# The merge of dilated attention: a power and all additions on GpSimd, and another place for the rows' tiles

## The chip, the core and the metric

The kernel runs on one core of a Trainium2 chip. A core has five engines that work at the same time, each through its own queue of instructions: TensorE (PE: matrix products; PEld is its loading of weights, which overlaps them), VectorE (DVE), ScalarE (ACT), GpSimd (POOL) and SyncE (SP, which here only issues DMA transfers). They share an on-chip memory of 128 partitions, in which every tile has its bytes in each partition; matrix products land in a separate small memory (PSUM), and DMA engines move data between the chip's memory and the main one. An instruction that needs another engine's result, or a buffer that another still uses, waits on a semaphore, and all that stands behind it in its engine's queue waits with it.

The metric is the time of one execution of the program on the device, in microseconds; lower is better.

## What is computed

One inference step of a hybrid decoder layer, for one prompt of 2048 tokens and for 32 sample tokens (8 requests of 4) that share its weights:

```python
a = rmsnorm(h); [qa|fa|ia|ga|qb|kb|vb] = a @ w_in
h = h + concat(HGRN2(qa,fa,ia,ga), DilatedAttn(qb,kb,vb)) @ w_o
h = h + ConvFFN(rmsnorm(h))
h = h + sigmoid(rmsnorm(h) @ w_ple_gate) * (p @ w_ple_proj)
```

The part at hand is the prompt's attention: 8 heads of 64 features, and three dilations (window, step): (128, 1), (512, 4) and (2048, 16). Each dilation gives, for every query, a maximum m of its scores, a sum l of their exponentials and a weighted sum acc of the values. They are combined so:

```python
w = exp(ms - ms.max(axis=0))
return (w[..., None] * accs).sum(0) / (w * ls).sum(0)[..., None]
```

## The kernel before

**Stages.** First the input projection, in two blocks of tokens, with the recurrent units (HGRN) between them; then the prompt's attention with the samples' work beside it; then the trunk (output projection, ConvFFN and embedding gate), in three blocks of tokens. The trunk's products are made of three matrix products each (lines 143 to 145), of weights and activations split into a rounded half and a remainder.

**The prompt's attention** (`attn_phase`). The heads are taken in four pairs, p = 0 to 3. The kernel folds the three dilations into two parts, di = 0 and di = 1, with a mask of counted entries, so two results per query are to be merged. A part of a pair has four chunks c of 512 tokens, a chunk four blocks of 128 queries, and a block one or two units. A unit makes scores (L811 and L812 on TensorE), adds the mask and finds the smallest sum (L816, one VectorE instruction; the sign is turned, so a smallest one stands for the maximum), takes exponentials on ACT (L817), turns them by transposes (L824), copies these out of PSUM (L826, on VectorE or for every fourth unit on ACT), and multiplies with the values (L836). When a chunk of a part is complete, ACT copies the result out of PSUM into a buffer `o0` or `o1`, five of each (L886).

TensorE's order in this stage is written out by hand: a loop over x steps through the units, and what is late by so many units is called at x - 3, x - 7 and so on. Between the units stands, every second turn, a piece of the samples' work (`others`), which reads 32 pieces of the cached keys and values of 1 MB each (tiles `skt`, L940 and L976).

**The next pair's data.** SP loads chunks of queries and keys into one of four `stage` buffers (L690). POOL rounds and subtracts them into `qS` (L701 and L149) and, after ACT has made `kH` (L704), into `kL` (L705). For p > 0 this happens about ten units before the pair begins.

**The merge** (`merge`, L740 to L775), once for each pair and chunk, 16 times in all, in six pieces that are called 0, 2, 3, 7, 10 and 11 turns after the chunk's second part. (1) SP loads the statistics of the first part back (L742). (2) VectorE takes the smaller of the two extremes (L750), POOL subtracts (L751), ACT takes exponentials (L752). (3) POOL multiplies and adds (L754, L755), VectorE takes the reciprocal of 128 x 8 values (L756), POOL multiplies (L757). (4) TensorE turns the coefficients (L760), ACT copies them out (L762), SP writes them to memory (L763) and loads them again, spread over the partitions, as `cf` (L767, two loads). (5) POOL multiplies the two results, 128 x 512 each, by their coefficients (L772). (6) The two are added (L774), by VectorE for p < 3 and by POOL for p = 3, and SP writes the sum to `mix_d` (L775).

**The seam to the trunk.** The trunk's first block loads pieces of w_o in halves, 128 x 512 each, into seven buffers `raw` (L1004). ACT rounds each (L181), VectorE makes the remainder (L182). The activations h are read from `mix_d` (L1098) and split the same way, by ACT in L1080 and VectorE in L1081. The weights are asked for first in each group of the program.

**What sets the order elsewhere.** Except for TensorE in the attention, a planner orders each engine's queue when the program is built, by a timeline that it computes itself. SP's queue is among those.

**Where tiles lie.** Pools are stacked in the on-chip memory in the order in which they are opened, and a pool that is closed gives its bytes to the next one opened. With `reuse_waits="tile"` a new tile waits only for the last users of those older tiles on whose bytes it lies. In front of all lies `const`, up to byte 4352 of a partition. Then come `early` (8448 bytes, with the mask from byte 6656 to 9728) and `rows` (two tiles of 4224 bytes, `ssq` and `rb`, used by the input projection's norm alone). Both are closed when attention ends. On their bytes the trunk opens `ffn_c` (the convolution's constants, 1952 bytes) and then `tr`, the seven `raw` buffers of 2048 bytes.

Of the kernel before, what the change touches and what calls it, by code (L numbers as in the profile page):

```python
# [11 lines left out]
F32 = mybir.dt.float32  # L12
# [4 lines left out]
ALU = mybir.AluOpType  # L17
# [30 lines left out]
def hymba_step_kernel(ctx: ExitStack, tc: tile.TileContext, I: dict, O: dict):  # L48
    nc = tc.nc
    V, A, G, PE, SP = nc.vector, nc.scalar, nc.gpsimd, nc.tensor, nc.sync  # L50

    const = ctx.enter_context(tc.tile_pool(name="const", bufs=1))
    dram = ctx.enter_context(tc.tile_pool(name="scratch", bufs=1, space=DRAM))

    early_st = ExitStack()
    early = early_st.enter_context(tc.tile_pool(name="early", bufs=1, reuse_waits="tile"))

# [15 lines left out]
    ones = const.tile([128, 128], F32, name="ones")  # L73
    V.memset(ones, 1.0)

    mask = early.tile([128, 768], F32, name="mask")
    qT_s = early.tile([128, 4, NS], F32, name="qT_s")
    kT_s = early.tile([128, 4, NS], F32, name="kT_s")
# [603 lines left out]
    def attn_phase(spare, rest):  # L682
# [57 lines left out]
        def merge(p, c, parts, both):  # L740

            SP.dma_start(both[:, 0].rearrange("p n h c -> p n (h c)"),  # L742
                         stats_d[p][512 * c:512 * c + 512].rearrange("(n i) c -> i n c", i=128))
            stats = both.rearrange("p i n h c -> p c h i n")
            spread = lambda x: x.rearrange("p h (o n) -> p h o n", o=1).to_broadcast([128, 2, 2, 4])
            yield
            mn = sm.tile([128, 2, 4], F32, name="mn")
            w = sm.tile([128, 2, 2, 4], F32, name="w")
            wl = sm.tile([128, 2, 2, 4], F32, name="wl")
            V.tensor_reduce(mn, both.rearrange("p i n h c -> p c h n i")[:, 1], axis=mybir.AxisListType.X, op=ALU.min)  # L750
            G.tensor_sub(w, spread(mn), stats[:, 1])  # L751
            A.activation(w, w, AF.Exp)  # L752
            yield
            G.tensor_mul(wl, w, stats[:, 0])  # L754
            G.tensor_add(mn, wl[:, :, 0], wl[:, :, 1])  # L755
            V.reciprocal(mn, mn)  # L756
            G.tensor_mul(w, w, spread(mn))  # L757
            yield
            ptr = pT.tile([128, 4, 128], F32, name="PT")[:16, 0]
            PE.transpose(ptr, w.rearrange("p h d n -> p (h d n)"), ident)  # L760
            wt = sm.tile([16, 128], F32, name="wt")
            A.copy(wt, ptr)  # L762
            SP.dma_start(coef_d[p][c], wt)  # L763

            cf = wk.tile([128, 2, 512], F32, name="cf", bufs=2)
            for h in range(2):
                SP.dma_start(cf[64 * h:64 * h + 64].rearrange("p d i -> p (d i)"),  # L767
                             coef_d[p][c][8 * h:8 * h + 8].rearrange("(o r) i -> o (r i)", o=1)
                             .to_broadcast([64, 1024]))
            yield  # L770
            for i in range(2):
                G.tensor_mul(parts[i], parts[i], cf[:, i])  # L772
            yield
            (G if p == 3 else V).tensor_add(parts[1], parts[1], parts[0])  # L774
            SP.dma_start(mix_d[:, 4 + p, 512 * c:512 * c + 512], parts[1])  # L775

        class Block:
# [71 lines left out]
        n = len(units)  # L849
# [5 lines left out]
        def merge_at(xs, *args):  # L855
            gen = merge(*args)
            for x in xs:
                at(x, lambda: next(gen, None))
# [702 lines left out]
    def step(gen, n):  # L1561
        for _ in range(n):
            if next(gen, "end") == "end":
                return False
        return True

    def pools(st, **kw):
        def pool(name, bufs, **k):
            return st.enter_context(tc.tile_pool(name=name, bufs=bufs, reuse_waits="tile", **kw, **k))
        return pool  # L1570

    rows_st, in_st, hgrn_st, attn_st = [ExitStack() for _ in range(4)]
    rows = pools(rows_st)("rows", 1)
    pool = pools(in_st)
    args = (in_tiles(pool("xp", 1), rows), [], pool("wp", 9), pool("ev", 2), pool("sm", 1),
            pool("pmm", 2, space=PSUM), pool("pms", 2, space=PSUM))
# [80 lines left out]
        first(side, 1000)  # L1657
    step(main, 1000)
    attn_st.close()
    rows_st.close()  # L1660

    early_st.close()
    with ExitStack() as st:
        pool = pools(st)
        cp = pool("ffn_c", 1)
# [153 lines left out]
```

## Time and profile before

| | us |
|---|---|
| time, median of 3 runs | 3003.89 (3002.21 to 3005.41) |
| the profiled execution: its own time | 3008.49 |
| the profiled execution: its span | 3006.7 |
| TensorE's mean granted clock in it | 0.981 of full speed |
| TensorE busy, 0 to 830 us (input projection, HGRN) | 798.0 of 830 |
| TensorE busy, 830 to 1200 us (attention, samples) | 336.2 of 370 |
| TensorE busy, 1200 to 3006 us (trunk) | 1774.7 of 1806 |

The profile is of one execution, taken by the hardware's profiler. Its span runs from the first to the last instruction; the execution's own time lies around it. Times of single instructions come from this execution, and "idle time" of an engine is set down with what ended it: the instruction or the transfer that released the semaphore last. An idle time of an engine that is not the bottleneck costs nothing by itself. The granted clock is what the throttle left to TensorE, as a share of full speed. The loss of 33.8 us in the attention's stretch is made of many short gaps, not of one.

### The profile page before, as it was taken

To read this page: it belongs to the slowest core of one execution; us is meant where nothing else is said; L and a number is where in the kernel's file an instruction comes from. 1 tells how busy PE (TensorE), PEld (TensorE's weight loads), DVE (VectorE), ACT (ScalarE), POOL (GpSimd) and SP (SyncE) were. 2 spreads that over 40 slices of the span, in tenths; PEclk is the share of its full clock that TensorE was granted. 3 is DMA by queue.
4 is the path that set the end of the run, shared out by engine and by line. 5 is a ranking of instruction groups with operands and counts; after the bars stand their busy time and mean duration, and the time that the engine had idled before them with its cause. 6 is when DMAs were issued, how large, how long until landed. Compare 5 with 4: busy or idle time off the path is not lost.

```text
span 3006.7 us, 52441 instructions
## 1 busy us (share of the span) xinstructions
PE 2908.9 (97%) x18895; PEld 2711.0 (90%) x18895; DVE 2166.4 (72%) x4717; ACT 1319.2 (44%) x2856; POOL 676.9 (23%) x792
## 2 busy tenths in 40 slices
PE   8999999999989998999999999999999999999998
PEld 8987789887777677999999999999999999999997
DVE  6656768657386567569988889766769777777777
ACT  5333433222176666335444444544444544444453
POOL 1443222212143463102344431000001000000000
PEclk9999999999989999999999999999999999999998
DMA  5898634323349996766666568677779777778773
GB/s 183 297 359 299 202 103 120 99 86 121 122 107 286 276 249 177 260 224 220 224 206 196 191 198 302 227 252 250 246 230 321 240 242 246 257 249 295 269 274 131
DMA packets 343061, 664.14 MB, mean 221 GB/s; under 512 B 62929, under 2 KB 130641, under 8 KB 341009
## 3 DMA queue, kind: packets, MB, share of 16 engines
q1 hardware_dynamic: 305952, 472.68, 48.4%
q0 software_dynamic: 33264, 121.13, 12.6%
q10 hardware_dynamic: 3584, 66.98, 6.1%
q8 instruction: 149, 2.44, 0.3%
q14 instruction: 112, 0.91, 0.1%
HBM read 513.72 MB, written 213.92 MB: 242 GB/s over the span
## 4 chain that ended last, share of the span: by engine, by line
PE 78%; DVE 9%; DMA 7%; issue 2%; ACT 2%; POOL 1%; SPq 1%; DVEq 0%; POOLq 0%; ACTq 0%
PE mm L143 19%; PE mm L144 19%; PE mm L145 19%; PE mm L345 2%; PE mm L346 2%; PE mm L347 2%; PE acc L836 2%; PE PT L824 2%; PE S L811 1%; DVE h L1305 1%; PE S L812 1%; PE lv L482 1%; DMA wraw<-in_w_in_dram 1%; DMA cf<-coef_d 1%; DMA draw<-in_w_down_dram 1%
## 5 line engine op out<-in xcount | busy, mean ns | idle before, releaser
L144 PE MATMUL mm<-w 128*128 128x348 f32 (+3 forms) x3636 | 1167.6, 322 | 1.9 <-DVE w L1081 1.1
L143 PE MATMUL mm<-w 128*128 128x348 f32 (+3 forms) x3508 | 1111.4, 323 | 21.2 <-ACT s L1247 6.7
L145 PE MATMUL mm<-w 128*128 128x348 f32 (+3 forms) x3508 | 1118.9, 322 | 0.7 <-DVE w L182 0.7
L144 PEld LDWEIGHTS mm<-w 128*128 128x128 f32 x3636 | 685.4, 189 | 4.9 <-DVE w L1081 3.0
L143 PEld LDWEIGHTS mm<-w 128*128 128x128 f32 x3508 | 658.2, 189 | 29.7 <-ACT s L1247 9.3
L145 PEld LDWEIGHTS mm<-w 128*128 128x128 f32 x3508 | 660.2, 189 | 1.8 <-DVE w L182 1.0
L182 DVE TENSOR_TENSOR w<-raw,w 128x512 fp32r<-128x512 f32 x586 | 420.8, 723 | 180.8 <-ACT w L181 175.7
L181 ACT CAST w<-raw 128x512 fp32r<-128x512 f32 x586 | 360.9, 621 | 414.5 <-PE mm L145 286.4
L1289 POOL DMA_DIRECT2D w<-wd_d x231 | 123.8, 536 | 900.1 <-PE mm L145 794.1
L1305 DVE TENSOR_TENSOR h<-h,mm 128x348 f32<-128x348 f32 (+1 forms) x504 | 248.7, 510 | 44.7 <-PE mm L145 43.1
L817 ACT ACTIVATE P<-P,st 128x256 f32<-128x256 f32 (+3 forms) x256 | 134.1, 526 | 67.2 <-DVE st L816 62.6
L1247 ACT COPY s<-mm 128x348 f32<-128x348 f32 (+1 forms) x198 | 87.9, 444 | 158.1 <-PE mm L145 158.0
L816 DVE CUSTOM_DVE_ANT_0 P<-S,mask 128x256 f32<-128x256 f32 (+3 forms) x256 | 104.4, 448 | 62.2 <-PE S L812 39.5
L345 PE MATMUL mm<-wh,xh 128*128 128x512 f32 x352 | 141.0, 404 | 0.0
L346 PE MATMUL mm<-wl,xh 128*128 128x512 f32 x352 | 140.5, 400 | 0.0
L347 PE MATMUL mm<-wh,xl 128*128 128x512 f32 x352 | 140.3, 399 | 0.0
L143 PE MATMUL mm<-xh,wh 128*128 128x384 f32 (+2 forms) x384 | 124.5, 328 | 7.0 <-ACT xh L243 5.0
L145 PE MATMUL mm<-xh,wl 128*128 128x384 f32 (+2 forms) x384 | 124.1, 328 | 4.7 <-DVE wl L268 4.6
L144 PE MATMUL mm<-xl,wh 128*128 128x384 f32 (+2 forms) x384 | 124.8, 327 | 1.3 <-DVE xl L244 1.2
L182 DVE TENSOR_TENSOR dw<-draw,dw 128x512 fp32r<-128x512 f32 x77 | 73.0, 954 | 52.7 <-ACT dw L181 52.6
L149 POOL TENSOR_SCALAR wh<-wraw 128x512 fp32r<-128x512 f32 x96 | 77.4, 820 | 131.6 <-PE mm L144 42.4
L268 DVE TENSOR_TENSOR wl<-wraw,wh 128x512 fp32r<-128x512 f32 x104 | 84.5, 833 | 28.6 <-POOL wh L149 23.3
(346 smaller groups left out, 5090.9 us busy)
## 6 DMA issues: line engine op xcount, KB each, us to landing
w<-wd_d POOLq DMA_DIRECT2D x231, 512.0 KB, 5.5
wd_d<-dw SPq DMA_DIRECT2D x77, 512.0 KB
out_sk_dram<-in_cache_k_dram ACTq DMA_DIRECT2D x56, 584.0 KB
out_sv_dram<-in_cache_v_dram ACTq DMA_DIRECT2D x56, 584.0 KB
raw<-in_w_gate_dram SPq DMA_DIRECT2D x110, 256.0 KB
raw<-in_w_up_dram SPq DMA_DIRECT2D x110, 256.0 KB
wraw<-in_w_in_dram SPq DMA_DIRECT2D x104, 256.0 KB
raw<-w_gate_d SPq DMA_DIRECT2D x88, 256.0 KB
```

The costliest lines, as they stand in the source:

```text
L143: PE.matmul(ps, lhsT=wh, rhs=xh, start=first, stop=False, skip_group_check=read)
L144: PE.matmul(ps, lhsT=wh, rhs=xl, start=False, stop=False, skip_group_check=read)
L145: PE.matmul(ps, lhsT=wl, rhs=xh, start=False, stop=last, skip_group_check=read)
L181: A.copy(w[:, 0], raw)
L182: V.tensor_sub(w[:, 1], raw, f32(w[:, 0]))
L345: PE.matmul(ps, lhsT=xh[k][:, js], rhs=wh, start=k == 0, stop=False)
L346: PE.matmul(ps, lhsT=xh[k][:, js], rhs=wl, start=False, stop=False)
L347: PE.matmul(ps, lhsT=xl[k][:, js], rhs=wh, start=False, stop=k == NK - 1)
L816: V.tensor_tensor_reduce(pe, s[:, w * i:w * i + w], bl.mask, 1.0, 3e38, ALU.add, ALU.min, mn)
L817: A.activation(pe, pe, AF.Exp, bias=mn, scale=-1.0, accum_out=st[:, bl.r, hh, 0:1])
L1289: G.dma_start(t, wd_d[p][n - 1])
L1305: V.tensor_add(o, o, acc[m][:, :H])
```

## The change

The division by the sum of weights becomes a power with exponent minus one, on GpSimd: a tile `minus` of 128 x 1 is filled with -1 at the start, and spread over the eight columns. The addition of the two weighted results goes to GpSimd for all four pairs. And the pool `rows` is opened ahead of `early`, so that it lies below it: its two tiles now take bytes 4352 to 12800, `early` follows, and the mask lies from byte 15104 to 18176, 8448 bytes higher than before (both but for the few bytes that `minus` takes in `const`). The order of closing follows: `early` first, then `rows`.

```diff
@@ start of the kernel @@
+    rows_st = ExitStack()
+    rows = rows_st.enter_context(tc.tile_pool(name="rows", bufs=1, reuse_waits="tile"))
     early_st = ExitStack()
     early = early_st.enter_context(tc.tile_pool(name="early", bufs=1, reuse_waits="tile"))
...
     ones = const.tile([128, 128], F32, name="ones")
     V.memset(ones, 1.0)
 
+    minus = const.tile([128, 1], F32, name="minus")
+    G.memset(minus, -1.0)
     mask = early.tile([128, 768], F32, name="mask")
@@ merge @@
             G.tensor_mul(wl, w, stats[:, 0])
             G.tensor_add(mn, wl[:, :, 0], wl[:, :, 1])
-            V.reciprocal(mn, mn)
+            inv = mn.rearrange("p h n -> p (h n)")
+            G.tensor_tensor(inv, inv, minus.to_broadcast([128, 8]), op=ALU.pow)
             G.tensor_mul(w, w, spread(mn))
...
             for i in range(2):
                 G.tensor_mul(parts[i], parts[i], cf[:, i])
             yield
-            (G if p == 3 else V).tensor_add(parts[1], parts[1], parts[0])
+            G.tensor_add(parts[1], parts[1], parts[0])
             SP.dma_start(mix_d[:, 4 + p, 512 * c:512 * c + 512], parts[1])
@@ opening and closing of the pools @@
-    rows_st, in_st, hgrn_st, attn_st = [ExitStack() for _ in range(4)]
-    rows = pools(rows_st)("rows", 1)
+    in_st, hgrn_st, attn_st = [ExitStack() for _ in range(3)]
...
     attn_st.close()
+    early_st.close()
     rows_st.close()
 
-    early_st.close()
     with ExitStack() as st:
```

## The prediction

> **What bounds the kernel now.** I began with the page: busy shares, then the chain that ended last.
>
> ```profile
> PE 2908.9 (97%) x18895; PEld 2711.0 (90%) x18895; DVE 2166.4 (72%) x4717; ACT 1319.2 (44%) x2856; POOL 676.9 (23%) x792
> PE 78%; DVE 9%; DMA 7%; issue 2%; ACT 2%; POOL 1%; SPq 1%; DVEq 0%; POOLq 0%; ACTq 0%
> ```
>
> TensorE is busy for 97% of the span, so about 98 us are all that any reordering could win. The change touches one stage, the prompt's attention (about 830 to 1213 us), and its seam with the trunk. I read the windows of that stage next, with one of the trunk. The columns are the stretch, then its length and each engine's busy time (PE, PEld, DVE, ACT, POOL), the granted clock, the DMA engines' busy share and GB/s.
>
> ```profile
> 900.00:950.00 50.00, 46.60 (x389) 35.54 (x389) 32.05 (x123) 34.07 (x103) 23.98 (x32) 0.94 0.97 289
> 950.00:1000.00 50.00, 45.81 (x417) 32.77 (x414) 29.95 (x95) 30.59 (x82) 22.46 (x23) 0.93 1.00 285
> 1000.00:1050.00 50.00, 44.67 (x352) 32.38 (x350) 22.97 (x92) 28.95 (x91) 18.46 (x26) 0.89 0.98 265
> 1050.00:1100.00 50.00, 49.55 (x465) 35.69 (x466) 32.98 (x112) 31.70 (x88) 29.54 (x32) 0.94 0.96 266
> 1250.00:1300.00 50.00, 50.00 (x324) 49.97 (x323) 29.04 (x54) 15.62 (x25) 0.00 (x0) 1.00 0.65 218
> ```
>
> From 900 to 1100 us TensorE idles 200 - 186.6 = 13.4 us, and the DMA engines are busy 96 to 100% of the time. In the trunk TensorE never idles, so a microsecond won before it stays won. The timeline then names the gaps that the merge and the seam own (start, length, engine, line, operation, and in brackets the idle time before it and who ended it):
>
> ```profile
> 964.54 2.49 POOL L772 TENSOR_TENSOR o<-o,cf 128x512 f32<-128x512 f32 x2 [23.88 <-DMA cf<-coef_d]
> 967.06 0.69 DVE L774 TENSOR_TENSOR o<-o,o 128x512 f32<-128x512 f32 x1 [4.98 <-POOL o L772]
> 967.79 1.07 ACT L886 COPY o<-acc 128x512 f32<-128x512 f32 x1 [4.70 <-DVE o L774]
> 968.50 1.94 PE L824 MATMUL PT<-c_ident,P 128*128 128x128 f32 x8 [3.36 <-DVE pt L826]
> 1194.74 0.28 PE L760 MATMUL PT<-c_ident,w 128*16 128x128 f32 x1
> 1201.56 0.66 PE L143 MATMUL mm<-w 128*128 128x348 f32 x1 [6.54 <-ACT w L1080]
> ```
>
> At 962 us VectorE reaches its addition L774 and stands there, because POOL's two products before it wait for the coefficients (cf) from memory. The transposed copies (L826) queue behind it, and TensorE stops for 3.36 us. ACT stands too: its copy L886 needs the buffer o that L774 reads last. The seam is the larger gap: 6.54 us before the trunk's first product.
>
> **The change, part by part.** First the operations (groups of instructions, 880 to 1215 us; busy us, mean ns, then idle time before them and its releaser).
>
> ```profile
> L774 DVE TENSOR_TENSOR o<-o,o 128x512 f32<-128x512 f32 x12 | 10.4, 865 | 15.8 <-POOL o L772 15.8
> L774 POOL TENSOR_TENSOR o<-o,o 128x512 f32<-128x512 f32 x4 | 6.2, 1543 | 0.2
> L756 DVE RECIPROCAL mn<-mn 128x8 f32<-128x8 f32 x16 | 3.1, 197 | 8.6 <-POOL mn L755 8.3
> L755 POOL TENSOR_TENSOR mn<-wl 128x8 f32<-128x8 f32 x16 | 3.5, 221 | 0.7
> L772 POOL TENSOR_TENSOR o<-o,cf 128x512 f32<-128x512 f32 x32 | 41.7, 1323 | 101.7 <-DMA cf<-coef_d 98.9 <-DMA mix_d<-o 2.7
> ```
>
> *Removed from VectorE:* 12 additions (10.4 us) and 16 reciprocals (3.1 us), with 15.8 + 8.6 us of standing before them: 37.9 us of its queue. *Added to POOL:* 12 x 1.54 = 18.5 us of additions and 16 powers. The trace shows no power on POOL. From below it is bounded by the 0.22 us of the 128x8 addition. From above: a 128x512 addition costs 1543 - 221 ns more for 504 more elements, 2.6 ns each, so a power worth a hundred additions would take 0.2 + 8 x 0.26 = 2.3 us; I keep 5 us as the far end, since a routine that works element by element isn't excluded. I take 0.9 us (thirty additions' worth, nearer the small row because only 8 columns are touched): 14 us in all. POOL was free for half of each stretch above, so its total of 33 us has room. The memset of minus one is a single small instruction at the start, beside the constants' loading: nothing.
>
> *What that is worth at 968 us.* The standing of VectorE goes, but not the reason for it. The buffer o is then released by POOL's addition, 1.54 us instead of 0.69 us after 967.03, so ACT's L886 ends its wait about 0.8 us later than now, with the exponentials behind it. The next thing late is the cache data (skt), which TensorE takes in a fixed order among the attention units:
>
> ```profile
> 973.85 5.04 SPq L976 DMA_DIRECT2D skt<-in_v_d_dram  x2
> 984.80 0.64 PE L979 MATMUL s<-skt,sPT 128*32 128x512 f32 x4
> 1040.50 0.39 SPq L940 DMA_DIRECT2D skt<-in_kT_d_dram  x1
> 1050.45 1.94 PE L942 MATMUL s<-skt,qb 128*32 128x512 f32 x8 [4.02 <-DMA skt<-in_kT_d_dram]
> ```
>
> The second pair prices such a load with the DMA engines full: 10 us from issue to use. By it the load issued at 973.85 lands at about 983.8, and is used at 984.80: one microsecond of slack. A TensorE that comes 3.4 us earlier waits here for 2.4. So of the gap I count 1.0 us as won; the bounds are 0.8 us lost and the whole 3.4 us.
>
> *The layout.* The trunk's pools begin where the constants end: 1952 bytes of ffn_c, then seven raw weight buffers of 2048. Until now the mask lies 2304 to 5376 bytes above that point, under the first two raw buffers; with rows (2 x 4224 bytes) below, it lies at 10752 to 13824, under the fifth and sixth. The rows tiles are last read when attention begins, at about 830 us. The seam, with SP's queue, the mask's last reader (L816) and ACT:
>
> ```profile
> 1189.20 0.42 DVE L816 CUSTOM_DVE_ANT_0 P<-S,mask 128x256 f32<-128x256 f32 x1
> 1189.65 0.81 SPq L1004 DMA_DIRECT2D raw<-in_w_o_dram  x2
> 1191.44 1.38 SPq L1004 DMA_DIRECT2D raw<-in_w_o_dram  x3
> 1193.53 1.09 SPq L767 DMA_DIRECT2D cf<-coef_d  x2
> 1194.67 2.20 SPq L1004 DMA_DIRECT2D raw<-in_w_o_dram  x3
> 1194.14 2.15 ACT L181 CAST w<-raw 128x512 fp32r<-128x512 f32 x3
> 1197.10 0.62 ACT L181 CAST w<-raw 128x512 fp32r<-128x512 f32 x1 [0.18 <-DMA raw<-in_w_o_dram]
> 1200.21 0.62 ACT L181 CAST w<-raw 128x512 fp32r<-128x512 f32 x1 [2.50 <-DMA raw<-in_w_o_dram]
> 1200.74 5.48 ACT L1080 CAST w<-h 128x696 fp32r<-128x696 f32 x8
> ```
>
> The first raw load goes out 0.03 us after the mask's last read, and the others stand behind it in SP's queue. ACT casts six raw halves before it casts h, and the sixth, issued in the group of 1194.67, lands at 1200.2; TensorE needs only the first two of them and h. With the first loads free of the mask they are out of that queue, and each later one moves up two places, past the cf loads of the last merges (256 KB each, issued after them instead of before: their products have until the trunk's second block). The sixth then goes out with the group of 1191.44, whose members were cast by 1197.72, so its cast follows at once: 1197.7 + 0.6, and h begins at 1198.3 instead of 1200.74. That is 2.4 us; if the planner, which orders these queues at build time, brings the first two casts before 1192 as well, 1.1 us more. I take 3.5 us. The lower bound is nothing (ACT keeps its order and some other load is the sixth), the upper one the 6.5 us of the gap.
>
> **Sum:** 1.0 + 3.5 = 4.5 us. The profiled execution took 3008.49 us, 1.8 around its span of 3006.7, so it would take 3004.0. It is 4.6 above the median of the three timed runs, 3003.89; against that median the forecast is 2999.4.
>
> **The rivals.** *A, TensorE gets all of it.* After the stall the clock drops:
>
> ```profile
> 968.00:972.00 4.00, 3.50 (x24) 2.87 (x28) 2.77 (x7) 2.98 (x6) 0.00 (x0) 0.50 1.04 235
> 972.00:976.00 4.00, 4.00 (x22) 2.07 (x18) 1.18 (x3) 0.44 (x1) 2.08 (x2) 0.73 1.07 260
> ```
>
> The clock column shows 0.50 and 0.73 of full speed, so 4 x 0.50 + 4 x 0.27 = 3.1 us of TensorE's work are lost on top of 3.4. If earlier issues make the loads earlier too, both come back and, with the seam's 3.5, the time is 3003.9 - 10.0 = 2993.9. For it speaks that TensorE works without a gap from 980 to 990 us; against it the DMA column. [...]
>
> *B, slower: POOL becomes late for the next head pair.* Its place is 1077 to 1105 us, where POOL turns the staged queries and keys into qS and kL and frees their stage buffers, between the merges of the pair before.
>
> ```profile
> 1080.00:1100.00 20.00, 20.00 (x198) 14.11 (x198) 13.48 (x55) 15.14 (x45) 19.69 (x24) 1.00 0.81 242
> 1092.53 3.08 POOL L705 TENSOR_TENSOR kL<-stage,kH 128x512 fp32r<-128x512 f32 x2
> 1103.02 1.23 SPq L690 DMA_DIRECT2D stage<-kT_d  x2
> 1103.97 0.48 PE L824 MATMUL PT<-c_ident,P 128*128 128x128 f32 x1 [3.51 <-ACT P L817]
> ```
>
> POOL is full there (19.69 of 20). SP refills the buffer that L705 leaves at 1095.6 only at 1103.0: 7.4 us of cover. Three additions and four powers in this burst cost 4.6 + 4 x 0.9 = 8.2 us: just at the edge, and the planner may put some behind L705. It decides from powers of about 0.7 us on if all stand ahead of L705. At 3 us each it is 16.6 - 7.4 = 9.2 us per burst, behind an already late TensorE (3.51 us), with SP's other loads queued behind. One such burst less the seam's gain gives 3003.9 + 9.2 - 3.5 = 3009.6; both bursts (the other at 980 to 1008) about 3019.
>
> *C, nothing.* The layout doesn't do what it says: the planner leaves the raw loads at the end, and the cache loads eat the rest. Time 3003.9, with the additions' 0.8 us either way.
>
> **How the numbers follow.** The forecast has 0.45, A 0.22, B 0.17, C 0.16. This kernel's measurement can tell about 0.2% from no change, 6 us: below 2997.9 is faster, above 3009.9 slower. A is faster for nearly all of its share (0.20); the forecast, with its bounds of -6.5 - 3.4 and +0.8, for a third (0.15). B is slower for most of its share (0.13); the rest, 0.52, is the same. The range takes in the forecast's bounds, C, most of A and B's single burst: 2992 to 3010.
>
> **What would show it.** Right: no VectorE instruction that waits for L772 or L755; L886 still waiting, now for POOL; the first raw loads ahead of the mask's last read, and L1080 near 1197; TensorE's gap at the seam near 3 us; cache waits longer by 1 to 3 us in 970 to 1050. A: no such waits, and no half clock after 968. B: SP's stage loads waiting for POOL, TensorE waiting for kH or kL at a pair's beginning, and powers of over 1 us. The forecast is wrong altogether if the build's plan moves other instructions in the attention stage by more than these few microseconds.

## The result, and the profile after

The changed kernel takes 3016.03 us (median of 5 runs, 3015.07 to 3018.74) against 3002.21 for the kernel before (5 runs, 2996.77 to 3005.41). The ratio is 1.0047, with a 95% interval of 1.0033 to 1.0061: some 14 us slower, outside the range given and on the other side of the forecast. The profiled execution after took 3016.26 us, with a span of 3014.5: 7.8 us above the one of before, which at 3008.49 us was slower than that kernel's median. So this pair of profiles shows only part of the 14 us.

The page of the changed kernel, its busy shares and its chain (its lines are numbered 4 to 5 higher than before):

```profile
PE 2906.0 (96%) x18895; PEld 2707.5 (90%) x18895; DVE 2157.0 (72%) x4689; ACT 1318.0 (44%) x2856; POOL 712.1 (24%) x821
PE 74%; DMA 10%; DVE 9%; issue 3%; ACT 2%; POOL 1%; SPq 1%; DVEq 0%; POOLq 0%; ACTq 0%
```

TensorE works as long as before; VectorE is busy for 9 us less, and GpSimd for 35 us more. What grew in the chain that ended last is the DMA, from 7 to 10%. The windows of the attention stage show the same (columns as above):

```profile
950.00:1000.00 50.00, 44.51 (x425) 31.85 (x418) 26.67 (x93) 31.68 (x85) 24.14 (x25) 1.00 1.00 287
1000.00:1050.00 50.00, 43.34 (x356) 31.07 (x354) 22.22 (x89) 27.46 (x87) 27.66 (x32) 0.93 1.00 253
1050.00:1100.00 50.00, 43.26 (x411) 31.60 (x411) 28.41 (x95) 31.51 (x87) 24.50 (x25) 0.97 1.00 246
1100.00:1150.00 50.00, 42.23 (x323) 35.05 (x316) 24.82 (x111) 28.23 (x92) 41.21 (x49) 0.76 0.80 198
```

From 1000 to 1100 us the DMA engines are wholly busy, and yet they move less: 253 and 246 GB/s, where it was 265 and 266 at 96 to 98%. From 1044 to 1130 us TensorE waits 7.8 us for the cache's tiles skt, where before it waited 4.0. TensorE executes the same instructions in the same order in both kernels, so each of its instructions can be set beside itself. How much later than before it starts (positive: the changed kernel is later), by the time of the instruction before the change:

```
at (us, before)    830   890   968   999  1044  1089  1104  1135  1180  1202  1217  1256
later by (us)     +0.8  -2.7  -3.0  -0.5  +0.4  +5.1  +1.7 +12.0 +11.5  +9.8  +8.1  +9.3
```

Up to 1044 us nothing is lost. Between there and 1135 us TensorE falls 11.5 us behind, and at the seam it wins 2 to 3 us back. (In the trunk another 4.5 us of this one pair of executions come back at about 1440 us, where the one of before had a wait of 2.4 us and after it a granted clock of 0.50 (1435 to 1440 us) and 0.77 (1440 to 1444), and the one of the changed kernel a wait of 1.3 us and a clock of 1.00 after it (1444 to 1453); 3.4 us of them are lost again by the end of the trunk.)

The groups of the moved operations (880 to 1230 us; busy us, mean ns, then idle time before them and its releaser):

```profile
L761 POOL TENSOR_TENSOR mn<-mn,minus 128x8 f32<-128x8 f32 x16 | 26.4, 1650 | 0.6
L779 POOL TENSOR_TENSOR o<-o,o 128x512 f32<-128x512 f32 x16 | 21.0, 1312 | 0.6
L891 ACT COPY o<-acc 128x512 f32<-128x512 f32 x29 | 23.4, 806 | 20.0 <-POOL o L779 17.3 <-PE acc L841 2.8
```

A power (L761) takes 1.65 us, between the bounds of 0.22 and 2.3 us but nearly twice the 0.9 I took; the additions (L779) take 1.31 us. And ACT's copy now stands for POOL's addition, as forecast.

### The profile page after: what moved, and what is told of

Its sections match the earlier page's. It is cut to its first block, busy times and chain, and to the rows that moved or that the text cites. A ratio compares the mean times of both kernels' runs of the same rounds, so it can differ in the third digit from the quotient of the medians.

```text
span 3014.5 us, 52433 instructions
## 1 busy us (share of the span) xinstructions
PE 2906.0 (96%) x18895; PEld 2707.5 (90%) x18895; DVE 2157.0 (72%) x4689; ACT 1318.0 (44%) x2856; POOL 712.1 (24%) x821
## 4 chain that ended last, share of the span: by engine, by line
PE 74%; DMA 10%; DVE 9%; issue 3%; ACT 2%; POOL 1%; SPq 1%; DVEq 0%; POOLq 0%; ACTq 0%
PE mm L147 19%; PE mm L149 18%; PE mm L148 18%; PE mm L349 2%; PE mm L350 2%; PE mm L351 2%; PE acc L841 1%; PE PT L829 1%; DMA skt<-in_v_w_dram 1%; PE S L816 1%; DMA v<-v_d 1%; DMA draw<-in_w_down_dram 1%; DVE h L1310 1%; DMA skt<-in_v_d_dram 1%; DMA xr<-in_xT_dram 1%
## 5 line engine op out<-in xcount | busy, mean ns | idle before, releaser
L816 PE MATMUL S<-kH,qS 128*128 128x256 f32 (+3 forms) x256 | 98.8, 401 | 6.1 <-DVE st L821 3.6
```

What stands on the lines that cost most here:

```text
L816: PE.matmul(s[:, w * i:w * i + w], lhsT=bl.q(hh), rhs=bl.k(kH, hh), start=True, stop=False)
```

## The experiments

Four theories were set against each other, under the letters of the expectations. **Q**: GpSimd's longer queue delays the next pair's loads, mostly by the additions. **P** (later D): the powers' own duration. **R**: the layout. **S**: the power's place in GpSimd's queue, whatever it takes. **L**, for e6 and e7 alone, says that the loss arises where GpSimd is full, ahead of the fourth pair, and the **B** beside it that both bursts of the merge lose. **M** came up with the results of e5 to e7: the tile `minus`, laid in the pool in front of all others, moves every later tile. All comparisons ran with 5 rounds beside the kernel before; "ratio" is to that.

### The parts alone: e1 to e4

```diff
e1: rows ahead of early, rows_st closed after early_st (as in the change), nothing else
e2: -(G if p == 3 else V).tensor_add(...)   +G.tensor_add(...)   nothing else
e3: -V.reciprocal(mn, mn)   +minus, memset, G.tensor_tensor(..., op=ALU.pow)   nothing else
e4: e2 and e3
```

Layout, e1:

> Only the place of the rows' tiles is changed; reciprocal and additions as before. Theory Q (the queue): the loss of the whole change comes from what GpSimd was given in the attention, and the layout is the part that wins at the seam; this kernel is 2 to 4 us faster than before, with the gap ahead of the trunk's first product down from 6.5 to about 4.5 us. Rival R (the layout loses): tiles at other addresses wait for other users; this kernel carries most of the 13.8 us, so plus 8 us or more. Rival P (the power): as Q here.

Additions, e2:

> Only the 12 additions go to GpSimd; reciprocal on VectorE, layout as before. Theory Q: SP's loads of the next pair's queries and keys are ordered behind GpSimd's longer queue and then stand in front of the cache loads; the additions are most of GpSimd's new time (12 x 1.3 to 1.5 us), so plus 6 to 12 us. Rival P (the powers of 1.65 us each, four in a burst, are the cost): minus 1 to plus 2 us. Rival R: about 0.

Power, e3:

> Only the reciprocal becomes a power on GpSimd; additions and layout as before. Theory Q: 16 x 1.65 us on GpSimd, less than the additions and without the buffers o behind them: plus 1 to 4 us. Rival P: 4 x 1.65 = 6.6 us in each of the two bursts ahead of a pair, so plus 6 to 13 us. Rival R: about 0.

Additions and power, e4:

> Additions and power on GpSimd, layout as before. Theory Q and rival P: the whole loss and no gain at the seam, so 14 to 18 us above before (the changed kernel's 13.8 and 2 to 4 of the seam). Rival R: within 4 us of before.

Measured: e1 3000.27 us (ratio 0.9988, 0.9977 to 0.9999), e2 3004.52 (1.0002, 0.9990 to 1.0013), e3 3017.25 (1.0039, 1.0025 to 1.0053), e4 3013.15 (1.0030, 1.0017 to 1.0043); before 3004.63. So R and Q fall: the layout wins 3.6 us (0.3 to 6.9), and the twelve additions show no cost (0.6 us, -3.0 to 3.9). All of the loss comes with the power's edit. The layout's gain is at the seam, where the queues of e1 differ from before; elsewhere they don't, but for two small loads and a fill of the trunk's constants that move up to 829 to 846 us. The timeline of e1 there:

```profile
1187.91 4.01 SPq L1006 DMA_DIRECT2D raw<-in_w_o_dram  x3
1191.14 0.42 DVE L818 CUSTOM_DVE_ANT_0 P<-S,mask 128x256 f32<-128x256 f32 x1
1199.08 0.62 ACT L183 CAST w<-raw 128x512 fp32r<-128x512 f32 x1 [0.53 <-DMA raw<-in_w_o_dram]
1199.76 5.48 ACT L1082 CAST w<-h 128x696 fp32r<-128x696 f32 x8
1200.58 0.95 PE L145 MATMUL mm<-w 128*128 128x348 f32 x2 [3.60 <-ACT w L1082]
```

The first raw loads go out 3.2 us ahead of the mask's last read, and TensorE's gap is 3.60 us instead of 6.54.

### Duration or place, and one pair at a time: e5 to e8

```diff
e5: e3 with op=ALU.mult in the place of op=ALU.pow
e6, e7: e3 with the power for p == 1 (e6) or p == 2 (e7) alone, V.reciprocal for the other pairs
e8: e1 and e2 (the change without the power)
```

e5 leaves the division out, so its coefficients are others; it serves for the time alone.

> As the kernel with the power alone, but GpSimd multiplies by minus one instead of raising to it: an instruction of the same tiles at the same place of the program, some 0.22 us instead of 1.65. The reciprocal is left out, so the coefficients are others. Theory D (the duration of the power is the cost): the 12 us of the power alone are gone, minus 2 to plus 3 us against before. Rival S (the step's place on GpSimd is the cost: it queues behind the next pair's preparation, whatever it takes itself): plus 8 to 12 us remain.

> The power on GpSimd only for the second of the four head pairs, the reciprocal on VectorE for the others. Theory L (the loss arises where GpSimd is full, ahead of the fourth pair, by the merges of the third): minus 3 to plus 3 us. Rival B (both bursts lose, as they delay the loads of the following pair): plus 4 to 7 us.

> The power only for the third pair, whose merges fall into the stretch in which GpSimd prepares the fourth. Theory L: four powers carry the whole loss, plus 8 to 12 us. Rival B: plus 4 to 7 us. If sixteen powers cost by their number, a quarter of 12: plus 3 us.

> The change without the power: additions on GpSimd, rows below the mask, reciprocal on VectorE. If the parts add up (layout 0.9988, additions 1.0002 of before): 0.999 of before, some 3 us faster. If the additions on GpSimd undo the layout's gain at the seam (GpSimd's last merges end there): about 0.

Measured beside 3001.71: e5 3015.59 us (1.0039, 1.0021 to 1.0057), e6 3014.68 (1.0043, 1.0027 to 1.0060), e7 3014.87 (1.0049, 1.0031 to 1.0067; one of its six runs took 12,086 us and is not in the ratio, and the median of the other five is 3011.70), e8 2999.07 (0.9998, 0.9989 to 1.0007). (The layout's gain isn't seen in e8, but 0.9988 x 1.0002 = 0.9990 lies inside its interval.) Within these intervals neither the time of the power nor the number of the powers matters: a multiplication (an estimate of 0.2 us, from the addition of its shape, 0.21 in the change), four powers at one place, or four at another, each shows about the loss of sixteen. S foresaw e5, but nothing foresaw both e6 and e7. What the change and the five slow kernels here (e3 to e7) share, and the three others (e1, e2, e8) lack, is the tile `minus`. It has 4 bytes per partition and takes 32 of them in `const`, which lies in front of everything. The values v then begin 32 bytes behind a multiple of 256 (byte 86816 of the partition, not 86784), and so do the stage buffers (21280, not 21248).

### The displacement alone, and the change without it: e9 to e13, e15b

```diff
e9:  before, + minus = const.tile([128, 1], F32); G.memset(minus, -1.0)      (used by nothing)
e10: the change, - const.tile([128, 1], ...)  + const.tile([128, 16], ...)[:, 0:1]   (64 bytes)
e11: the change, + a pool with a tile [128, 8] between a_r and a_w           (32 bytes ahead of v, P, pt, o, cf)
e12: e3 with the tile of 64 bytes
e13: the change with const.tile([128, 64], ...)[:, 0:1]                      (256 bytes)
e15b: e3 with the tile of 256 bytes
```

> The kernel before with nothing of the change but the tile for minus one (128 x 1, filled once, used by nothing). It moves every later tile by 32 bytes, so that tiles which began at a multiple of 64 bytes, the values v among them, no longer do. Theory M (the moved addresses are the cost, by slower DMA pieces of 512 bytes): plus 10 to 13 us. Rival S (the step's place on GpSimd is the cost): 0, minus 2 to plus 2 us.

> The whole change, each instruction in the same order as there, but the tile for minus one takes 64 bytes instead of 4 (rounded to 32), so later tiles keep their place within 64 bytes. Theory M: the loss is gone, minus 4 to plus 1 us against before, and the 512-byte DMA pieces between 900 and 1195 us take 41 us of 16 engines again and not 45.5. Rival S: plus 12 to 15 us as the change itself.

> The whole change with the small tile, and 32 bytes of padding ahead of the attention's pool of v, P, pt, o and cf: those (and what follows them) are where they were within 64 bytes, while stage, qS, kH and kL in front of them stay displaced. Theory M with v as the tile that counts: minus 4 to plus 2 us against before. M with the stage tiles as those that count: plus 10 us or more. Rival S: plus 12 to 15 us.

> The power alone (reciprocal on GpSimd), in the same order of instructions as in its first run, with the tile for minus one padded to 64 bytes. Theory M: 0, minus 2 to plus 3 us against before: the power by itself costs next to nothing. Rival S: plus 12 us.

> The whole change, the tile for minus one padded to 256 bytes, so that the values v begin at a multiple of 256 bytes as before (padded to 64 they began 64 bytes behind one). If a start at 64 bytes is all that counts: as with 64, 1.0011 of before, plus 1 to 5 us. If a start at 256 bytes counts: as the sum of the parts without displacement, layout minus 4 and additions 0 and a power that is cheaper than thought, so 2 to 5 us below the run with 64 and about 0 against before.

> The power alone, tile padded to 256 bytes; the control for the other two. If 64 bytes are all that counts: 1.0023 of before again, plus 5 to 9 us. If 256 count: plus 1 to 4 us.

Measured beside 3004.21: e9 3009.02 us (1.0014, 1.0001 to 1.0026), e10 3006.84 (1.0011, 1.0000 to 1.0022), e11 3010.50 (1.0024, 1.0010 to 1.0038), e12 3012.65 (1.0023, 1.0010 to 1.0037). Beside 3002.72: e13 3004.23 (1.0005, 0.9992 to 1.0018), e15b 3006.39 (1.0013, 1.0001 to 1.0025).

M as first worded, with a multiple of 64 as what counts, missed: e10, e11 and e12 stand 3, 7 and 7 us above before, and at most 1, 2 and 3 were expected if v counts. So the padding of e13 and e15b is 256, which brings v back to a multiple of 256; a start 128 bytes behind one was not tried. e10 and e13 have every instruction of the change in the same order on every engine; only addresses differ. Padding to 256 bytes takes the ratio from 1.0047 to 1.0005, 12.6 us of 14.1 (about 7 to 18 by the two intervals). With 256 as the multiple, M carries the main part. Alone, in e9, the displacement costs 4 us (0.3 to 7.8), less than M had said and more than S. The windows of e13, beside those of the change above:

```profile
1000.00:1050.00 50.00, 46.60 (x385) 33.73 (x387) 24.99 (x96) 28.63 (x91) 28.53 (x33) 0.93 0.97 273
1050.00:1100.00 50.00, 45.04 (x445) 32.76 (x443) 30.63 (x109) 32.41 (x92) 31.56 (x33) 1.00 0.96 265
```

273 and 265 GB/s, at a smaller share; TensorE's waits for skt from 1044 to 1130 us are 2.9 us there. The DMA view of 900 to 1195 us shows it in one line (packets, MB, share of 16 engines), first before, then the change, then e13:

```profile
q1 hardware_dynamic: 63683, 71.77, 86.7%
```

```profile
q1 hardware_dynamic: 60969, 69.72, 89.7%
```

```profile
q1 hardware_dynamic: 63340, 71.25, 86.3%
```

295 us x 0.897 / 69.72 MB is 3.80 us per MB in the change, and 295 x 0.863 / 71.25 = 3.57 in e13; before has 3.56. The other kernels with equal orders and other addresses go the same way: e3 3.67 and e15b 3.55, e5 3.74 and e14 3.58, e9 3.67 and before 3.56. The packets' own records say which pieces: those of 512 bytes, of which the values v are some 12,300 of 21,000 (mean ns from 900 to 1195 us, by where v begins modulo 256):

```
v begins at 0:    before 31.7  e1 32.9  e2 31.7  e8 31.3  e13 31.6  e14 32.7  e15b 32.0  e16 32.5  e18 32.1
v begins at 64:   e10 33.4  e11 33.6  e12 34.3
v begins at 32:   change 35.1  e3 35.1  e4 35.1  e5 35.2  e6 35.5  e7 33.9  e9 34.6  e17 35.0
```

Over 20 executions the first group stands clear of the other two, which just overlap. About 21,000 pieces x 3.5 ns / 16 engines are 4.6 us of DMA time. The pieces of 2048 bytes take longer too: 115.9 ns in the change against 109.6 in e13, 110.4 in e3 against 107.3 in e15b, 112.9 in e5 against 108.1 in e14, 110.6 in e9 against 108.6 before. But their means overlap from kernel to kernel (112.7 in e1, where v and stage are not displaced), so what share of the loss is theirs is not shown. (One execution doesn't fit the sum: the profiled one of e1, its slowest of 12, has 3.68 us per MB with v at 0.)

### What the power itself costs, and which tiles count: e14, e16, e17

```diff
e14: e5 with the tile of 256 bytes (without the division, as there)
e16: e15b, and merge_at([x + d for d in ((0, 2, 3, 7, 10, 11) if p == 3 else (0, 2, 3, 9, 12, 13))], ...)
e17: e13, + the 32 bytes between a_r and a_w of e11
```

> GpSimd multiplies where the power stood (0.22 us instead of 1.65; the reciprocal is left out), tile padded to 256 bytes. Theory D (duration): minus 2 to plus 2 us against before. Rival S (the place in GpSimd's queue): as the power with the same padding, plus 5 to 8 us.

> As the power alone with 256 bytes, but for the first three pairs TensorE's transposition of the coefficients, and what follows it, stands two turns (about 5 us) later in TensorE's order. If TensorE's waits for the coefficients (for L760 and for ACT's copy of them) are the power's price: those waits are gone between 1100 and 1140 us and the time is 3 to 7 us below the control. Rival: the loads of the next pair are late whatever the coefficients do: as the control, or slower, as the buffers o are held longer.

> The whole change padded to 256 bytes as in e13, but with 32 bytes of padding ahead of the attention's pool of v, P, pt, o and cf, so that these (and what follows them) are displaced while stage, qS, kH and kL are not. If the values' 512-byte pieces carry the loss: 1.003 to 1.005 of before, and 512-byte pieces of 34 to 36 ns on average between 900 and 1195 us. If the stage tiles carry it: 1.0005 as e13. If both: in between, 1.002.

Measured beside 3002.72: e14 3004.46 us (1.0004, 0.9991 to 1.0016), e16 3007.80 (1.0021, 1.0007 to 1.0034). Beside 3003.74: e17 3009.16 (1.0026, 1.0014 to 1.0037).

e14 against e5 (1.0039) is a third pair of kernels with equal orders and other addresses, and S falls with it: at that place a short operation shows no cost (1.2 us, -2.7 to 4.8). The power by itself is 1.0013, 4 us (interval 0.3 to 7.5), in e15b. It shows as waits of TensorE between 1090 and 1140 us, first in e15b, then in e16 (in total, times, longest); those for the coefficients, `wt` and `w`, are 7.8 us in e15b and 0.2 in e14:

```profile
PE PT L827 <- ACT wt L765: 6.1, 2, 4.3
PE PT L827 <- DVE hsat L617: 2.3, 1, 2.3
PE PT L763 <- POOL w L760: 1.7, 1, 1.7
```

```profile
PE PT L827 <- ACT P L820: 2.6, 1, 2.6
PE s L614 <- POOL hsF L605: 1.9, 1, 1.9
PE s L614 <- DVE hsF L426: 1.4, 1, 1.4
```

Moving the transposition two turns later removes the waits for the coefficients, and the time doesn't fall (1.0021 against 1.0013). So taking these waits away wins nothing here. Whether they only took the place of others, or the buffers o held two turns longer cost what was won, isn't separated. e17 displaces v, its pool and the attention's tiles behind it (skt from 32 to 64 behind a multiple of 256) and loses 0.0021 of 0.0042. e11, which moves the same tiles on from 32 to 64 (skt to 96), wins 0.0023. Between them, v and the tiles behind it carry about half, as closely as these intervals tell; the rest is with the tiles in front or those of the trunk, and no tile was tried by itself.

### A kernel that beats both: e18

```diff
e1, + s_pad: a tile [128, 56] ahead of s_c (skt then begins at 0 modulo 256, not 32)
    + a tile [128, 24] at the start of ffn_c (raw begins at 0, not 160)
```

> The layout alone, with padding that brings the cache's tiles skt and the trunk's raw buffers, 32 and 160 bytes behind a 256-byte multiple until now, to such a multiple; v and stage stay at theirs. If every piece loses by its start: 3 to 8 us faster than before, more than the layout alone (0.9988), and 2048-byte pieces under 108 ns between 900 and 1195 us. If pieces of 2048 bytes don't care: 0.9988 again, 2 to 5 us faster than before.

Measured: 2991.94 us (10 runs, 2984.46 to 2997.74) against 3003.74, ratio 0.9967 (0.9955 to 0.9979): 12 us by the medians, 10 by the ratio (6 to 14), faster than before, more than either expectation, and 24 faster than the change, which was measured beside other runs of before. In all other kernels here the cache's tiles began 32 to 96 bytes behind a multiple of 256. Windows of e18:

```profile
950.00:1000.00 50.00, 49.27 (x483) 35.90 (x482) 34.14 (x115) 36.32 (x103) 29.89 (x34) 1.00 1.03 310
1050.00:1100.00 50.00, 46.62 (x421) 33.03 (x419) 31.85 (x110) 35.90 (x102) 32.79 (x38) 0.96 0.96 266
```

310 GB/s in a stretch that had 285, and 2048-byte pieces of 106.6 ns (median 84) from 900 to 1195 us instead of 112.7 (median 88) in e1. (The mean of e1 is that of its slowest execution; the other kernels with v at 0 have 107.3 to 109.7, so it is the median, 87 or 88 in them, that stands apart.) The order of every engine's instructions is that of e1 but for the two fills. What skt and what raw wins of it, and what the other tiles that the padding moves, wasn't separated; TensorE is 6.5 us ahead of before already at 1180 us, before the trunk, where e1 was 2 behind.

## Why the prediction was wrong, step by step

**The step that failed** is the one that cost nothing: "The memset of minus one is a single small instruction at the start, beside the constants' loading: nothing." The instruction is (0.1 us); its tile is not. It moves every later tile off its start, in a stage in which I had myself shown the DMA engines 96 to 100% busy. What it costs is 1.0047 - 1.0005 = 0.0042, 12.6 us. The layout's bytes were worked out for the mask and the raw buffers, and the same sum would have shown that v leaves a multiple of 256, though not what that costs.

**The power's price** was mis-sized (0.9 us taken, 1.65 measured), but that is not the loss. Rival B foresaw a loss at the right place, but its mechanism (GpSimd late, so the stage loads late) isn't what the main loss comes from. The profile of the change does show its signs:

```profile
1101.84 1.22 SPq L694 DMA_DIRECT2D stage<-kT_d  x2
1108.18 2.10 ACT L708 CAST kH<-stage 128x512 fp32r<-128x512 f32 x2 [4.16 <-DMA stage<-kT_d]
1110.16 1.22 SPq L694 DMA_DIRECT2D stage<-kT_d  x2
1110.83 0.44 PE L829 MATMUL PT<-c_ident,P 128*128 128x128 f32 x2 [4.31 <-ACT P L822]
1116.40 2.15 ACT L708 CAST kH<-stage 128x512 fp32r<-128x512 f32 x2 [3.08 <-DMA stage<-kT_d]
1119.52 1.12 PE L829 MATMUL PT<-c_ident,P 128*128 128x128 f32 x4 [1.92 <-ACT wt L767]
```

The last two groups of kT loads go out 5.4 and 7.1 us later than before (there at 1096.49 and 1103.02), and TensorE stands behind ACT, which stands until they land. But in e13, with the same queues, the last goes out at 1101.45 us:

```profile
1101.45 1.22 SPq L694 DMA_DIRECT2D stage<-kT_d  x2
```

So the length of GpSimd's queue alone did not make them late. With powers of 1.65 us B's own sum gives 4.6 + 4 x 1.65 - 7.4 = 3.8 us for a burst. The 4 us of the power alone (e15b) don't contradict that size, but they are a third of the loss at most, and most of the waits shown there are for the coefficients, none for qS, kH or kL.

**The gain at 968 us** came and went as the forecast had it. The timeline of the change (start, length, idle time before in brackets):

```profile
966.84 1.27 POOL L779 TENSOR_TENSOR o<-o,o 128x512 f32<-128x512 f32 x1
968.15 1.10 ACT L891 COPY o<-acc 128x512 f32<-128x512 f32 x1 [4.54 <-POOL o L779]
969.28 0.69 DVE L821 CUSTOM_DVE_ANT_0 P<-S,mask 128x512 f32<-128x512 f32 x1 [2.04 <-ACT o L891]
977.30 1.06 PE L984 MATMUL s<-skt,sPT 128*32 128x512 f32 x8 [0.53 <-DMA skt<-in_v_w_dram]
```

ACT stands for GpSimd's addition, VectorE for ACT, and TensorE, 3.0 us earlier than before, comes to wait for skt. Rival A's sign is there as well: the granted clock stays at 1.00 from 968 to 976 us, where it was 0.50 and 0.73, so that TensorE goes from 0.5 us late at 960 us to 4.3 early at 977. But up to 1000 us it waits 3.9 us for skt, where before it did not at all, and is 0.5 us early at 999: 1.0 us won in all, as counted, and A's 6.5 (3.4 of standing and 3.1 by the clock) not kept. What I didn't see is that the rest is taken as well when the fourth pair begins. In e2, the additions alone, TensorE stands 5.9 us at about 1102 us behind ACT, which had stood for the fourth pair's loads, and 4.3 us at 1127 us for VectorE; it is 8.7 us ahead of before at 1104 us and 0.3 behind at 1135, and the ratio is 1.0002.

**The seam** was right in sign and nearly in size: 3.5 us forecast, 3.6 measured in e1 (0.3 to 6.9), though its gap alone shrank by 2.9. So near a hit is luck in part: the interval is wide, and the order differs from the one I drew. The cf loads still go out ahead of the last raw group, and the sixth half still lands late (0.53 us of wait, instead of none). In the change itself the gap is 4.49 us:

```profile
1209.81 0.62 ACT L185 CAST w<-raw 128x512 fp32r<-128x512 f32 x1 [1.58 <-DMA raw<-in_w_o_dram]
1211.31 0.95 PE L147 MATMUL mm<-w 128*128 128x348 f32 x2 [4.49 <-ACT w L1085]
```

**The sum** with measured terms: layout -3.6, additions +0.6, power +4, displacement +12.6, together +13.6 us; measured +14.1 by the ratio. The last term is itself the change less e13, so what this sum tests is only that the other three come to e13's +1.5 (they give +1.0). Against the forecast's -4.5 the displacement is the largest part of the miss, and the power the next.

**What stays open.** The displacement costs 1.0014 where nothing else is changed (e9), and 0.0026 to 0.0042 between the pairs e3 and e15b, e5 and e14, the change and e13. The intervals nearly meet, so I can't say whether an order that is already tight loses more by it. Whether the power's 4 us are its duration (e14 is 1.0004, with an overlapping interval) is not settled either, nor is why a displaced piece takes longer (no record shows the inside of a transfer), nor which tiles carry the half that is not with v and those behind it.

## What to carry to other kernels

Where a stage keeps the DMA engines busy throughout, as this one did from 900 to 1100 us (96 to 100% before), the byte at which a tile begins can be part of its price: 32 bytes cost 4 us alone (e9) and 8 to 13 between kernels of equal orders (e3 and e15b, the change and e13). Work out the starts of all tiles before and after an edit, also of an edit that only adds a constant, and keep those with small pieces at multiples of 256, the fastest start of the three that v had here (or pad the small constant, as here; putting it last was not tried). When several unlike edits all cost the same, look for what they share besides their purpose. And give an edit costed at nothing the same test as the others: what does it move?

## What the runs showed of the hardware

- Pieces of 512 bytes, more than half of them into v, took 31.3 to 32.9 ns on average where v begins at a multiple of 256, 33.4 to 34.3 at 64 behind one, and 33.9 to 35.5 at 32 behind one. The 64-byte and the 32-byte ranges just overlap, so no order between these two is shown.
- The power on GpSimd took 1.65 us for 128 x 8 values in the change (L761), where an addition of that shape took 0.21 us (L759): 1.44 us more, 0.18 us for each of the eight columns by division, with no other width run.
